# A hybrid attention and state space layer: the two gates are computed inside the state space stage, in a written-out order

## The chip, the cores and the metric

One Trainium2 chip, of which the kernel uses one core. The metric is the device time in microseconds (us) of one execution of the program, the median over repeated runs. TensorE (PE) multiplies, VectorE (DVE), ScalarE (ACT) and GpSimd (POOL) work element by element, SyncE (SP) issues the DMAs.

## The reference, cut to what matters

One layer over 1024 tokens of width 1024, all in float32:

```
xn = RMSNorm(h)
z  = xn @ W_in  -> [q | k | v | gate_attn | u_ssm | gate_ssm]     (each 512 wide)
attn = dilated_window_attention(q, k, v) * silu(gate_attn)         (8 heads of 64)
ssm  = S5(u_ssm) * silu(gate_ssm)                                  (32 groups of 16 channels, 64 complex states)
h  = h + concat(attn, ssm) @ W_out
h  = h + sigmoid(RMSNorm(h) @ W_g) * (p @ W_p)
```

S5 is a diagonal complex recurrence along the tokens: per group an input matrix, a scan, an output matrix, a skip term, then GELU and a gated linear unit.

## The kernel before, in words

The program is one function, `hybrid_layer`, unrolled completely. A scheduler sorts the instructions before the run: each engine gets a fixed order, chosen from each instruction's priority (its place in the program text, moved ahead by `tc.high_priority(offset=...)`) and from the times at which its own clock model believes that operands are ready. `AHEAD` is such an offset. Nothing is reordered on the chip: an engine whose next instruction waits, waits.

Every large product is done in three matmuls (`mm3`, L109 to L112): high part times high part, low times high, high times low. A weight block of 512 columns comes in eight pieces (`load_w`, L149 to L165): a DMA into one of three raw buffers, the high part copied by ACT (L160), the low part subtracted by DVE or POOL (L161; a string such as `GL = "QV"` says who: Q is POOL, V is DVE). The eight pieces have eight buffers (`wp`), so a block's piece can be loaded when the last matmul of the block before it that uses this piece is done.

The stages, in the order of the text:

- **u** (L193 to L235): x comes in, is split into `xh` and `xl`, and u = W_in(2048..) x is accumulated. `stats` (L179) makes 1/rms of every token from the squares: as a column per token block (`rcol`, L182 to L185) and, through the PE, as a row on all partitions (`rrow`, L189 to L191). Beside it DVE computes the small parameters of the state space part (L247 to L415).
- **state space** (L437 to L603): u is scaled by `rrow` into `ust` (L445, half by POOL, half by DVE) and goes through memory into another layout, `ut` (L510). Then 32 groups are handled in eight halves of four groups: index f (0 to 3) times h2 (0, 1). `ssm_kernels(f)` builds for both halves of f the matrices `g` (L477 to L479) and `cpw` (L482 to L484); the PE transposes g into the bank `gp` (L493) and multiplies into the bank `kp` (L489); ACT copies `gt` (L496); the convolution matrix goes through memory into `wt` (L504). `ssm_scan` makes a phase table `tc`, `tf` (L531 to L535), the PE product `vp` (L540), and on DVE and POOL the products, the scan (L548) and `xpv` (L555). `ssm_out` sums three products per group into `yp` (L570 to L572) and ACT applies GELU (L574); `ssm_store` transposes on the PE (L581) and stores. The loop at L589 to L602 runs nine steps: scan of half i, output of half i-1, and at every even i the kernels of the next f.
- **gates** (L606 to L615): first gate_ssm (columns 2560..), then gate_attn (columns 1536..). Each is eight tiles (4 feature blocks f, 2 token halves n) of 24 matmuls (`feat_tile`, L420) in the PSUM tag `big`, which has two banks. DVE multiplies a tile by `rrow` (L613) into a buffer of the tag `ev`, which has four buffers and which the eight `ust` tiles use as well; ACT applies SiLU in place (L614); a DMA stores it (`sg_s`, `sa_s`). These matmuls come later in the text than the state space stage, so the scheduler may put them into its gaps.
- **q, k, v, attention, GLU, output products, second gate** (L620 to the end). The first matmuls of q stand right behind the gates. In `attention`, `output(b)` (L730 to L740) takes the finished token block b: a DMA loads its gate `ga` from `sa_s` (feature by token, 512 byte pieces), the PE transposes the block (L736) into a bank of the tag `t` (two banks), DVE multiplies it by the gate, ACT copies the high part (L709) and POOL subtracts the low part (L710, by `EA`).

Of the kernel before, what the change touches and what calls it, by code (L numbers as in the profile page):

```python
# [15 lines left out]
OP = mybir.AluOpType  # L16
# [9 lines left out]
GL = "QV"  # L26
UE = "QV"
# [32 lines left out]
SB = (2, 1, 1, 1, 4, 6, 4, 6)  # L60
# [20 lines left out]
def hybrid_layer(ctx: ExitStack, tc: tile.TileContext, a: dict, dbg=None):  # L81
    nc = tc.nc
    V, A, Q, T = nc.vector, nc.scalar, nc.gpsimd, nc.tensor
# [21 lines left out]
    sa_s = dr.tile([512, S], F32, name="sa_s")  # L105
# [73 lines left out]
    def stats(ss, name, out_col, out_row):  # L179
# [5 lines left out]
        V.tensor_copy(out_col, r)  # L185
        for n in range(2):
# [280 lines left out]
    def ssm_kernels(f):  # L467
        wt = s2.tile([P, 8, P], F32, tag="wt", name=f"wt{f}", bufs=SB[1])
        fr = slice(f * P, (f + 1) * P)
        gts, cps = [], []  # L470
        kp = bank("pv", f"kp{f}")
        for h2 in range(2):
            gs = slice(8 * f + 4 * h2, 8 * f + 4 * h2 + 4)
            nm = f"_{f}{h2}"
            g = q4("g" + nm, (P, 4, 8, 16), "g", SB[2])
            w = q4("gw" + nm, (P, 4, 9, 16), "cw", SB[3])
            Q.tensor_tensor(g, over_l(rows(pa, 0, 8, gs), 8), over_c(ba[:, gs], 8), op=OP.mult)  # L477
            E[SE[0]].tensor_tensor(w[:, :, 0:8], over_l(rows(pb, 0, 8, gs), 8), over_c(bb[:, gs], 8), op=OP.mult)
            E[SE[1]].tensor_tensor(g, g, w[:, :, 0:8], op=OP.add)  # L479
            cpw = q4("cp" + nm, (P, 4, 9, 16), "cp", SB[4])  # L480
            w = q4("cw" + nm, (P, 4, 9, 16), "cw", SB[3])
            Q.tensor_tensor(cpw, over_l(rows(pa, 0, 9, gs), 9), over_c(cre[:, gs], 9), op=OP.mult)  # L482
            E[SE[2]].tensor_tensor(w, over_l(rows(pb, 0, 9, gs), 9), over_c(cim[:, gs], 9), op=OP.mult)
            E[SE[3]].tensor_tensor(cpw, cpw, w, op=OP.add)  # L484
            cps.append(cpw)
            for j in range(4):
                A.activation(bm[h2][:, j, 16 * j:16 * j + 16], g[:, j, 0, :], AF.Copy)
            for j in range(4):
                T.matmul(kp[64 * h2:64 * h2 + 64, 0:P], bm[h2][:, j, :],  # L489
                         cpw[:, j, 0:8, :].rearrange("p l c -> p (l c)"), start=j == 0, stop=j == 3)  # L490
            gp = bank("t", "gp" + nm)
            for j in range(4):
                T.transpose(gp[:, j * P:(j + 1) * P], g[:, j].rearrange("p l c -> p (l c)"), ident)  # L493
            gt = [q4(f"gt{ri}" + nm, (P, 4, P), "gt", SB[5]) for ri in range(2)]
            for ri in range(2):
                A.activation(gt[ri].rearrange("p g (u s) -> p g u s", u=2),  # L496
                             gp.rearrange("p (g s) -> p g s", g=4)[:, :, 64 * ri:64 * ri + 64].unsqueeze(2)
                             .to_broadcast([P, 4, 2, 64]), AF.Copy)
            gts.append(gt)
        stt(kz[:, 112:128], eye16, dsk[:, f:f + 1], kp[:, 0:16], OP.mult, OP.add)  # L500
        A.activation(kz[:, 128:240], kp[:, 16:P], AF.Copy)
        nc.sync.dma_start(k_s[fr], kz)
        for jr in range(8):
            nc.sync.dma_start(wt[16 * jr:16 * jr + 16],  # L504
                              k_s[fr, 16 * jr:16 * jr + P].rearrange("(g c) f -> c g f", c=16))
        return gts, cps, wt
# [7 lines left out]
    def ssm_scan(f, h2, gts, cps, ut):  # L514
        g0 = 8 * f + 4 * h2
        gs = slice(g0, g0 + 4)
        nm = f"_{f}{h2}"
        gt, uth = gts[h2], ut[:, 4 * h2:4 * h2 + 4]
# [17 lines left out]

        vp = [bank("s", f"vp{ri}" + nm) for ri in range(2)]
# [52 lines left out]
    for i in range(9):  # L590
# [5 lines left out]
        if i:  # L596
# [4 lines left out]
            if h2:  # L601
                ssm_store(f, ygt[f])  # L602
# [496 lines left out]
```

## Time and profile before

| what | value |
|---|---|
| median of 3 runs | 697.68 us (694.65 to 699.17) |
| the profiled execution, its own time | 699.63 us |
| its span, first to last instruction | 697.9 us |
| mean granted TensorE clock | 0.965 of full speed |
| busy PE, DVE, ACT, POOL | 643.9, 454.4, 293.1, 298.2 us |
| instructions | 11020 |

All times below are on the axis of the profiled execution, us from the start of its span. A busy PE is not a PE at its peak: the ends of matmuls are modelled, and neighbours overlap. So the pace of a run of matmuls is read from the distance between the starts of two of them. PE matmuls in full float32 stand as two instructions each.

### The profile page before, as it was taken

What the parts mean: (1) busy time and instruction counts of PE and PEld (TensorE: products, weight loads), DVE (VectorE), ACT (ScalarE), POOL (GpSimd) and SP (SyncE); (2) the same over time, 40 slices, a digit from 0 to 9 for tenths busy, and PEclk for the clock granted to TensorE, in tenths of its full rate; (3) what the DMA queues carried; (4) which work ended last, traced back from release to release, by engine and by line L of the source; (5) the groups of instructions that cost most, each with busy time, mean ns of one, the idle gap of its engine ahead of it and who ended that gap; (6) DMA issues with size and microseconds to landing.
All of it is one profiled execution on the core that took longest, in us unless ns stands there. A gap on an engine that the chain in (4) does not pass through costs nothing.

```text
span 697.9 us, 11020 instructions
## 1 busy us (share of the span) xinstructions
PE 643.9 (92%) x3964; PEld 508.5 (73%) x3964; DVE 454.4 (65%) x916; ACT 293.1 (42%) x568; POOL 298.2 (43%) x259
## 2 busy tenths in 40 slices
PE   9999498779799999999999789889999999999997
PEld 6877387668688888887767466557677888888786
DVE  5999799978721347667563899966944765625222
ACT  7532152666841323337542665533622456103210
POOL 4425855877610212314242764622332436343631
PEclk9989799999999999999999979888999999999999
DMA  7804521244854315744671868798996344014101
GB/s 250 239 7 122 147 95 53 67 53 103 177 69 68 112 64 117 181 91 104 162 131 36 217 154 156 183 216 184 215 231 221 113 150 125 27 62 152 60 31 60
DMA packets 158118, 87.25 MB, mean 125 GB/s; under 512 B 117232, under 2 KB 130416, under 8 KB 158064
## 3 DMA queue, kind: packets, MB, share of 16 engines
q1 hardware_dynamic: 158064, 86.56, 51.3%
q8 instruction: 31, 0.51, 0.3%
q14 instruction: 23, 0.19, 0.1%
HBM read 48.81 MB, written 17.27 MB: 95 GB/s over the span
## 4 chain that ended last, share of the span: by engine, by line
PE 57%; DVE 19%; DMA 10%; issue 5%; POOL 4%; ACT 4%; SPq 0%; DVEq 0%; POOLq 0%; ACTq 0%
PE gt L111 4%; PE gt L112 4%; PE gt L110 4%; PE g L111 3%; PE g L112 3%; PE g L110 3%; DMA pt<-hl 3%; DMA wr<-in_w_in 2%; PE q L111 2%; PE q L112 2%; PE q L110 2%; PE os L110 2%; PE os L112 2%; PE os L111 2%; PE oa L110 2%
## 5 line engine op out<-in xcount | busy, mean ns | idle before, releaser
L161 POOL TENSOR_TENSOR wl<-wr,wh 128x512 fp32r<-128x512 f32 x34 | 48.0, 1411 | 114.1 <-ACT wh L160 59.6
L160 ACT ACTIVATE wh<-wr 128x512 fp32r<-128x512 f32 x68 | 42.2, 626 | 51.9 <-DMA wr<-in_w_in 24.1
L783 POOL TENSOR_TENSOR hl<-p,hl 128x384 f16<-128x384 f32 (+2 forms) x34 | 39.5, 1165 | 55.4 <-ACT hl L780 17.1
L110 PE MATMUL g<-xh,wh 128*128 128x512 f32 x128 | 52.5, 410 | 10.9 <-DVE gate L613 9.8
L776 ACT ACTIVATE p<-p,st 128x384 f32<-128x384 f32 (+4 forms) x64 | 39.8, 622 | 42.1 <-DVE st L753 42.0
L111 PE MATMUL g<-xl,wh 128*128 128x512 f32 x128 | 52.8, 412 | 0.0
L112 PE MATMUL g<-xh,wl 128*128 128x512 f32 x128 | 52.4, 409 | 0.0
L110 PE MATMUL gt<-hh,wh 128*128 128x512 f32 (+1 forms) x136 | 51.8, 382 | 0.1
L111 PE MATMUL gt<-hl,wh 128*128 128x512 f32 (+1 forms) x136 | 51.7, 381 | 0.0
L112 PE MATMUL gt<-hh,wl 128*128 128x512 f32 (+1 forms) x136 | 51.2, 383 | 0.0
L161 DVE TENSOR_TENSOR wl<-wr,wh 128x512 fp32r<-128x512 f32 x34 | 30.4, 893 | 28.0 <-ACT wh L160 23.3
L989 ACT ACTIVATE gg<-gg 128x512 f32<-128x512 f32 (+1 forms) x17 | 10.1, 606 | 66.6 <-DVE gg L286 66.5
L110 PEld LDWEIGHTS g<-xh,wh 128*128 128x128 f32 x128 | 25.0, 195 | 17.1 <-DVE gate L613 10.2
L991 POOL TENSOR_TENSOR gg<-gg,hs 128x512 f32<-128x512 f32 x14 | 18.1, 1297 | 43.0 <-DVE gg L286 41.4
L613 DVE TENSOR_TENSOR gate<-g,rrow 128x512 f32<-128x512 f32 x16 | 10.9, 684 | 36.0 <-PE g L112 32.1
L286 DVE TENSOR_TENSOR gg<-gt,rrow 128x512 f32<-128x512 f32 (+1 forms) x17 | 10.8, 656 | 32.8 <-PE gt L112 32.7
L753 DVE CUSTOM_DVE_ANT_0 p<-sc,mask,gc 128x128 f32<-128x128 f32 (+3 forms) x56 | 24.3, 458 | 9.0 <-PE sc L766 5.5
L110 PEld LDWEIGHTS gt<-hh,wh 128*128 128x128 f32 x136 | 25.6, 188 | 5.8 <-ACT wh L163 0.5
L111 PEld LDWEIGHTS gt<-hl,wh 128*128 128x128 f32 x136 | 25.6, 188 | 5.4
L112 PEld LDWEIGHTS gt<-hh,wl 128*128 128x128 f32 x136 | 25.6, 188 | 5.4
L111 PEld LDWEIGHTS g<-xl,wh 128*128 128x128 f32 x128 | 25.1, 196 | 5.8 <-issue 0.3
L112 PEld LDWEIGHTS g<-xh,wl 128*128 128x128 f32 x128 | 24.9, 195 | 5.6
(300 smaller groups left out, 1949.5 us busy)
## 6 DMA issues: line engine op xcount, KB each, us to landing
wr<-in_w_in SPq DMA_DIRECT2D x48, 256.0 KB, 3.3
xr<-in_x SPq DMA_DIRECT2D x16, 256.0 KB, 5.0
wr<-in_w_out SPq DMA_DIRECT2D x16, 256.0 KB, 3.6
xos<-in_x SPq DMA_DIRECT2D x16, 256.0 KB, 4.1
h_s<-xos SPq DMA_DIRECT2D x16, 256.0 KB, 3.7
xoa<-h_s SPq DMA_DIRECT2D x16, 256.0 KB, 2.8
wr<-in_w_ple_gate SPq DMA_DIRECT2D x16, 256.0 KB, 3.0
out_t<-gg SPq DMA_DIRECT2D x15, 256.0 KB, 2.0
```

The costliest lines, as they stand in the source:

```text
L110: T.matmul(o, lh, rh, start=first, stop=False)
L111: T.matmul(o, lh, rl, start=False, stop=False)
L112: T.matmul(o, ll, rh, start=False, stop=last)
L160: A.activation(hi, raw, AF.Copy)
L161: E[lo_on[k % len(lo_on)]].tensor_tensor(lo, raw, hi.bitcast(F32), op=OP.subtract)
L286: V.tensor_tensor(o, x, y, op=op)
L613: V.tensor_tensor(gt_, o, rrow[:, n * 512:(n + 1) * 512], op=OP.mult)
L753: V.tensor_tensor_reduce(out, sc, msk, gm, init, op0=OP.add, op1=OP.min, accum_out=acc_[:, hd:hd + 1])
L776: A.activation(pb_, pb_, AF.Exp, bias=mx[:, hc], scale=-1.0, accum_out=dn[:, hc])
L783: E[LE[b][h0 % len(LE[b])]].tensor_tensor(hl[:, na:2 * na], pr_[:, 0:na], hl[:, 0:na], op=OP.subtract)
L989: A.activation(gt_, gt_, AF.Sigmoid)
L991: (V if last else Q).tensor_tensor(gt_, gt_, hs, op=OP.add)
```

## The change

1. **A fixed order for TensorE.** A small class stands in front of the tensor engine; while `T.held` is true, every matmul and transpose is told to keep the order of the text. It is set before the first gate tile and cleared after the state space loop.
2. **The gates move into the stage.** A generator `gates()` makes one piece per call: first gate_attn in seven pieces (token blocks 0 and 1 together, then 2 to 7), then gate_ssm in eight tiles. `fill()` calls it: once before the rows of 1/rms are made, three times before `ust`, once between the kernels of halves 0 and 1, once in each step of the loop, once more in steps 0 and 1.
3. **gate_attn token by token.** Its tiles have tokens on the partitions (`tok_tiles`), so 1/rms is a scale per partition, and ACT applies it with SiLU straight from PSUM; `sa_s` is stored by token block. Its eight low parts of weights are all POOL's (`GLA = "Q"`).
4. **1/rms in two pieces.** `stats_cols` stays where it was, ahead; `stats_rows` comes after the first piece of gate_attn, with no raised priority.
5. **The loop per half.** `ssm_kernels` is cut into `kern_build(i)` (POOL, DVE, ACT) and `kern_pe(i)` (PE and the copies behind it); the table is its own function; a half's kernels are built two steps ahead and its table one step ahead.
6. **Buffers.** `gt` from 6 to 4, the shared work tag `tt` from 6 to 8.
7. **In `output(b)`** POOL multiplies the token block by the gate ahead of the transposes (`EA`), and DVE subtracts the low part from PSUM afterwards.

```diff
+    class T:
+        held = False
+        @staticmethod
+        def matmul(*args, **kw):
+            i = nc.tensor.matmul(*args, **kw)
+            if T.held:
+                tc.keep_in_program_order(i)
...
+    def gates():
+        w = [load_w(wp, a["w_in"], k, 1536, lo=GLA) for k in range(KT)]
+        for bs in ((0, 1), (2,), (3,), (4,), (5,), (6,), (7,)):
+            for b, o in zip(bs, tok_tiles(w, bs, [f"ga{b}" for b in bs], "big")):
+                gt_ = ev(f"gate_a{b}")
+                with tc.high_priority(offset=AHEAD):
+                    A.activation(gt_, o, AF.Silu, scale=rcol[:, b:b + 1])
+                nc.sync.dma_start(sa_s[b], gt_)
+            yield
+        w = [load_w(wp, a["w_in"], k, 2560, lo=GL) for k in range(KT)]
+        for f in range(4):
+            for n in range(2):
+                o = feat_tile(w, f, n, "big", f"gs{f}{n}")
...
+    T.held = True
+    fill()
+    stats_rows("st1", rcol, rrow)
...
+    fill(3)
     for f in range(4):
         ust = [ev(f"ust{f}{e}", (P, 4, P)) for e in range(2)]
...
+    gcp = {i: kern_build(i) for i in range(2)}
+    tabs = {0: table(0)}
+    inp = {0: ssm_inputs(0)}
+    gt = {0: kern_pe(0, *gcp[0])}
+    fill()
+    gt[1] = kern_pe(1, *gcp[1])
     for i in range(9):
         if i < 8:
-            xpv[i] = ssm_scan(f, h2, *ker[f][:2], inp[f])
-            if not h2 and f < 3:
-                ker[f + 1], inp[f + 1] = ssm_kernels(f + 1), ssm_inputs(f + 1)
+            f = i // 2
+            if i % 2 == 0 and f < 3:
+                inp[f + 1] = ssm_inputs(f + 1)
+            vp3 = scan_pe(i, gt[i], inp[f])
+        fill()
+        if i < 8:
+            xpv[i] = ssm_scan(i, vp3, *tabs[i], gcp[i][1])
+        if i + 2 < 8:
+            gcp[i + 2] = kern_build(i + 2)
+        if i + 1 < 8:
+            tabs[i + 1] = table(i + 1)
         if i:
...
+            ssm_out(f, h2, xpv[i - 1], ygt[f], gcp[i - 1][1], inp[f], wts[f])
             if h2:
                 ssm_store(f, ygt[f])
+        if i < 2:
+            fill()
+        if i + 2 < 8:
+            gt[i + 2] = kern_pe(i + 2, *gcp[i + 2])
+    fill(16)
+    T.held = False
     sp.close()
-    for c0, dst in ((2560, sg_s), (1536, sa_s)):
-        w = [load_w(wp, a["w_in"], k, c0, lo=GL) for k in range(KT)]
...
-            nc.sync.dma_start(gl, sa_s.rearrange("(r p) t -> p r t", p=P)[:, :, b * P:(b + 1) * P])
+            nc.sync.dma_start(gl, sa_s[b].rearrange("p (r t) -> p r t", r=4))
+            E[EA[b % 2]].tensor_tensor(at_, at_, gl, op=OP.mult)
             tp = bank("t", f"at{b}").rearrange("p (r t) -> p r t", t=P)
             for j in range(4):
                 T.transpose(tp[:, j], at_[:, j], ident)
-            tt(gl, tp, gl, OP.mult)
...
-            split(*(t_[:, b % 4] for t_ in ma[n]), gl.rearrange("p r t -> p (r t)"), E[EA[b % 2]])
+            split(*(t_[:, b % 4] for t_ in ma[n]), tp.rearrange("p r t -> p (r t)"), V)
```

`kern_pe(i)` issues the four transposes into `gp`, the two copies `gt`, then the eight matmul instructions into `kp`, and for odd i the stores and loads that make `wt`. `scan_pe(i)` issues the sixteen matmul instructions into `vp`. The engines that do the element work of a half (`SE`) are unchanged.

## Rows read from the trace of the kernel before

**Rows 1.** The page, part 1: busy us, share of the span, instructions.

```profile
PE 643.9 (92%) x3964; PEld 508.5 (73%) x3964; DVE 454.4 (65%) x916; ACT 293.1 (42%) x568; POOL 298.2 (43%) x259
```

**Rows 2.** Busy time by stage: stretch, length, engines' busy us, clock, DMA, GB/s.

```profile
94.00:192.00 98.00, 82.44 (x526) 70.79 (x525) 82.84 (x101) 61.05 (x126) 69.01 (x58) 0.97 0.42 86
192.00:238.00 46.00, 46.00 (x228) 38.20 (x227) 8.77 (x14) 13.06 (x21) 5.45 (x6) 1.00 0.45 73
238.00:345.00 107.00, 107.00 (x478) 85.53 (x477) 66.08 (x193) 48.44 (x95) 30.55 (x26) 1.00 0.53 121
345.00:530.00 185.00, 167.25 (x1693) 120.41 (x1692) 136.73 (x324) 85.42 (x190) 79.57 (x63) 0.94 0.79 174
```

**Rows 3.** Timeline of TensorE, last run of u: start, us, instruction.

```profile
48.15 0.40 PE L110 MATMUL u<-xh,wh 128*128 128x512 f32 x1
...
58.19 0.39 PE L111 MATMUL u<-xl,wh 128*128 128x512 f32 x1
```

**Rows 4.** The tile q: matmul ns min/median/max, first and last start.

```profile
L110 PE MATMUL q<-wh,xh x64: 391/397/400, 238.1 to 282.4; 128*128 128x512 f32 x64
```

**Rows 5.** Waits of TensorE from 58 to 240: us in total, times, longest.

```profile
PE g L110 <- DVE gate L613: 9.8, 1, 9.8
PE kp L489 <- DVE cp L484: 8.9, 5, 3.8
PE yt L581 <- ACT ygt L574: 3.5, 1, 3.5
```

**Rows 6.** Busy time around the longest wait: columns as in Rows 2.

```profile
72.50:83.77 11.27, 1.50 (x7) 0.88 (x6) 7.46 (x21) 0.88 (x1) 9.61 (x7) 0.78 0.52 153
83.77:94.00 10.23, 10.23 (x34) 8.13 (x35) 10.13 (x11) 2.20 (x7) 6.96 (x6) 0.74 0.59 191
```

**Rows 7.** Timeline of TensorE: the small products of the state space stage.

```profile
94.19 0.60 PE L493 MATMUL gp<-ident,g 128*128 128x128 f32 x4
...
96.11 1.09 PE L489 MATMUL kp<-cp,bm 128*64 128x128 f32 x8
...
121.50 1.95 PE L540 MATMUL vp<-ut,gt 128*128 128x128 f32 x16
...
195.02 0.38 PE L570 MATMUL yp<-wt,ut 128*128 128x128 f32 x2
...
200.15 0.39 PE L572 MATMUL yp<-cpi,xpv 128*128 128x128 f32 x2
...
205.50 1.03 PE L581 MATMUL yt<-ident,ygt 128*128 128x128 f32 x8
```

**Rows 8.** Groups of DVE from 58 to 240: busy us, mean ns, idle before.

```profile
L548 DVE TENSOR_TENSOR_SCAN y<-magp,w 128x128 f32<-128x128 f32 x32 | 14.0, 496 | 2.4 <-POOL xpv L554 2.4
...
L613 DVE TENSOR_TENSOR gate<-g,rrow 128x512 f32<-128x512 f32 x16 | 10.9, 684 | 36.0 <-PE g L112 32.1 <-POOL g L477 3.8
...
L161 DVE TENSOR_TENSOR wl<-wr,wh 128x512 fp32r<-128x512 f32 x9 | 7.4, 824 | 9.2 <-ACT wh L160 9.2
...
L286 DVE TENSOR_TENSOR wf<-vp,tf 128x512 f32<-128x512 f32 x8 | 5.5, 683 | 0.9 <-ACT tf L535 0.6 <-PE vp L540 0.3
```

**Rows 9.** Groups of POOL from 58 to 240, columns as in Rows 8.

```profile
L161 POOL TENSOR_TENSOR wl<-wr,wh 128x512 fp32r<-128x512 f32 x9 | 12.3, 1362 | 48.2 <-PE g L111 37.3 <-ACT wh L160 11.0
...
L445 POOL TENSOR_TENSOR ust<-uraw,rrow 128x256 f32<-128x256 f32 x8 | 11.2, 1426 | 4.6 <-DVE rrow L191 3.1 <-DMA u_s<-ust 1.6
```

**Rows 10.** Timeline of ACT: one change of its function table.

```profile
143.02 1.28 ACT L614 ACT_TABLE_LOAD   x1
144.31 0.63 ACT L614 ACTIVATE gate<-gate 128x512 f32<-128x512 f32 x1
```

**Rows 11.** The tile ga, the attention gate: ns min/median/max, first and last start.

```profile
L286 DVE TENSOR_TENSOR ga<-at,ga x8: 678/689/693, 393.9 to 525.6; 128x512 f32<-128x512 f32 x8
...
L710 POOL TENSOR_TENSOR mal<-ga,mah x8: 1282/1298/1672, 440.8 to 527.1; 128x512 fp32r<-128x512 f32 x8
```

**Rows 12.** Waits of DVE from 340 to the end.

```profile
DVE ga L286 <- DMA ga<-sa_s: 5.5, 3, 2.2
```

More of the change, by code (lines that the diff above doesn't have):

```diff
@@ L26 @@
 GL = "QV"
+GLA = "Q"
 UE = "QV"
@@ L233, in hybrid_layer, with feat_tile, ev, wa @@
     with tc.high_priority(offset=AHEAD):
-        stats(ss, "st1", rcol, rrow)
+        stats_cols(ss, "st1", rcol)
         V.tensor_tensor(rsq_, rcol, rcol, op=OP.mult)
+    def feat_tile(w, f, n, tag, name):
+        o = bank(tag, name)
+        c = slice(n * 512, (n + 1) * 512)
+        for k in range(KT):
+            mm3(o, w[k][0][:, f * P:(f + 1) * P], w[k][1][:, f * P:(f + 1) * P],
+                xh[k][:, c], xl[k][:, c], k == 0, k == KT - 1)
+        return o
+    def ev(name, shape=(P, 512)):
+        return rp.tile(list(shape), F32, tag="ev", name=name, bufs=4)
+    def wa(name, shape, dt=F32):
+        return rp.tile(list(shape), dt, tag="wa", name=name, bufs=2)
+    def wb(name, shape, dt=F32):
+        return wbp.tile(list(shape), dt, tag="wb", name=name, bufs=2)
+    def tok_tiles(w, bs, names, tag):
+        os_ = [bank(tag, name) for name in names]
+        for k in range(KT):
+            for o, b in zip(os_, bs):
+                c = slice(b * P, (b + 1) * P)
+                mm3(o, xh[k][:, c], xl[k][:, c], w[k][0], w[k][1], k == 0, k == KT - 1)
+        return os_
+    def gates():
[11 more added lines that the diff above has]
+                o = feat_tile(w, f, n, "big", f"gs{f}{n}")
+                gt_ = ev(f"gate_s{f}{n}")
+                with tc.high_priority(offset=AHEAD):
+                    V.tensor_tensor(gt_, o, rrow[:, n * 512:(n + 1) * 512], op=OP.mult)
+                    A.activation(gt_, gt_, AF.Silu)
+                nc.sync.dma_start(sg_s[f * P:(f + 1) * P, n * 512:(n + 1) * 512], gt_)
+                yield
+    gates_ = gates()
+    def fill(n=1):
+        for _ in range(n):
+            next(gates_, None)
+    T.held = True
+    fill()
+    stats_rows("st1", rcol, rrow)
     def p16(name):
@@ L465, in over_c @@
         return x.unsqueeze(2).to_broadcast([P, 4, n, 16])
-    def ssm_kernels(f):
-        wt = s2.tile([P, 8, P], F32, tag="wt", name=f"wt{f}", bufs=SB[1])
-        fr = slice(f * P, (f + 1) * P)
[L470 to L506, printed above, removed]
@@ new lines, in kern_pe @@
+    def kern_pe(i, g, cpw):
+        f, h2 = divmod(i, 2)
+        nm = f"_{f}{h2}"
+        fr = slice(f * P, (f + 1) * P)
+        gp = bank("t", "gp" + nm)
+        for j in range(4):
+            T.transpose(gp[:, j * P:(j + 1) * P], g[:, j].rearrange("p l c -> p (l c)"), ident)
+        gt = [q4(f"gt{ri}" + nm, (P, 4, P), "gt", SB[5]) for ri in range(2)]
+        for ri in range(2):
+            A.activation(gt[ri].rearrange("p g (u s) -> p g u s", u=2),
+                         gp.rearrange("p (g s) -> p g s", g=4)[:, :, 64 * ri:64 * ri + 64].unsqueeze(2)
+                         .to_broadcast([P, 4, 2, 64]), AF.Copy)
+        if not h2:
+            kps[f] = bank("pv", f"kp{f}")
+        kp = kps[f]
+        for j in range(4):
+            T.matmul(kp[64 * h2:64 * h2 + 64, 0:P], bm[h2][:, j, :],
+                     cpw[:, j, 0:8, :].rearrange("p l c -> p (l c)"), start=j == 0, stop=j == 3)
+        if h2:
+            stt(kz[:, 112:128], eye16, dsk[:, f:f + 1], kp[:, 0:16], OP.mult, OP.add)
+            A.activation(kz[:, 128:240], kp[:, 16:P], AF.Copy)
+            nc.sync.dma_start(k_s[fr], kz)
+            wts[f] = s2.tile([P, 8, P], F32, tag="wt", name=f"wt{f}", bufs=SB[1])
+            for jr in range(8):
+                nc.sync.dma_start(wts[f][16 * jr:16 * jr + 16],
+                                  k_s[fr, 16 * jr:16 * jr + P].rearrange("(g c) f -> c g f", c=16))
+        return gt
@@ L511, in ssm_inputs, with table @@
         return ut
[L514 to L518, printed above, removed]
+    def table(i):
+        gs = slice(4 * i, 4 * i + 4)
+        nm = f"_{i // 2}{i % 2}"
         tc_, tf = q4("tc" + nm, tag="e", bufs=SB[6]), q4("tf" + nm, tag="e", bufs=SB[6])
```

79 lines of the change are left out of this document (39 added, 40 removed).

## The prediction

> **What bounds the kernel now.** I read the page first: TensorE is busy for 92% of the span and every other engine for two thirds or less [rows 1]. That says which engine matters, but not where it loses time, so the next view is the busy time by stage. From 238 to 345 TensorE is busy in every microsecond, at clock 1.00; from 192 to 238 too, while DVE does 8.77 us of work in 46 [rows 2]. From 94 to 192 it is busy 82.4 of 98, and DVE 82.8 of 98 as well. So there are two pieces of one large stage: first the state space work, where DVE sets the pace and gate matmuls fill TensorE's gaps only in part, then the rest of the gates, where TensorE is alone. Work that TensorE does in that tail could have stood in the gaps in front of it.
>
> How large are the gaps? The pace of the big matmuls: from 48.15 to 58.19 lie 43 steps, 0.2335 us each [rows 3]. One more matmul follows, so u ends at about 58.65, and q begins at 238.1 [rows 4]: the stage lasts 179.4 us. TensorE's work in it, at full pace:
> - gates: 16 tiles of 24 matmuls, 384 x 0.2335 = 89.7;
> - `yp`: 195.02 to 200.15 are 23 steps of a pair, 0.223 each; 12 pairs a half, 2.68; eight halves 21.4 [rows 7];
> - a pair lasts 0.38, so one instruction lasts 0.27 beyond the start of the last. `vp`, 16 instructions at 0.1115: 1.78, by eight 14.3. `kp`: (1.09 - 0.27)/7 = 0.117, eight of them 0.94, by eight 7.5. `gp`: (0.60 - 0.27)/3 = 0.11, four 0.44, by eight 3.5. `yt`: (1.03 - 0.27)/7 = 0.109, eight 0.87, by four 3.5. The rows of 1/rms, 16 instructions at the pace of `kp`: 1.9.
>
> The sum is 141.8, so 37.6 us of the stage are not work. The three longest of ten kinds of waits are 9.8 for a gate tile's DVE multiply, 8.9 for DVE's sum `cp`, 3.5 for GELU [rows 5]. The rest is small waits and slow clock: after the 9.8 us the granted clock averages 0.74 over 83.77 to 94, part of it at the lower level of 1.2 GHz, and 34 matmuls that need 7.9 us take 10.2 [rows 6].
>
> **The change, part by part.** I follow TensorE, whose order is now the order of the text, and put a wait wherever the next instruction can be late.
>
> Start. Blocks 0 and 1 of gate_attn (48 matmuls, 11.2 us) come right behind u. They need the two `big` banks, which ACT has to empty, and weights whose low parts are now POOL's alone: eight by 1.36 = 10.9 us where POOL had four [rows 9], while DVE is rid of four by 0.82 [rows 8]. Value 3 us of wait, between 0 and 7 (five extra subtractions on POOL if all of it showed). End 72.9. Then the rows of 1/rms, 1.9: 74.8, later than before, when nothing stood between u and them. What hides that: `ust` needs them, 8 by 1.43 = 11.4 us on POOL [rows 9], which ends near 87; then half 0's `g` and `cp` follow, near 92. TensorE meanwhile does blocks 2 to 4 (16.8 us), until 91.6. The 9.8 us wait can't come back here: SiLU now reads PSUM itself, DVE's multiply L613 is gone for gate_attn (8 by 0.684 = 5.5 us off DVE, rows 8), and its `ev` buffers are asked for ahead of `ust`'s.
>
> Kernels 0 and 1 with block 5 between: 1.4 + 5.6 + 1.4. If POOL is late with `ust`, the wait falls here: value 2, between 0 and 5. End 102.
>
> Loop. 38.3 of the 141.8 are then done, 103.5 are left. A step with kernels takes TensorE 1.78 + 5.6 + 2.68 + 0.44 + 1.38 = 11.9 us; steps 0 and 1 have a gate tile more. DVE's nine groups of a half (the eleven rows from the scan to `wf`, without L613 and L161) sum to 87.5 us, 10.9 a half [rows 8], and with a gate tile's 0.68 it is 11.6. So the two engines are level, and DVE's own gaps decide. Before, DVE was busy for 85% of 94 to 192 [rows 2]; at that share a half would take 11.6/0.85 = 13.6, 1.7 more than TensorE's, in the four steps 2 to 5 together 6.8. Steps 0, 1, 6 and 7 have room (more matmuls there, or less DVE work). Value 6, between 0 (the two-step lead covers it) and 15 (twice that share of gaps). The buffers `g` and `cw` stay single, so DVE can't run further ahead; that excludes a gain beyond 0.
>
> The weights change once inside the loop, from gate_attn to gate_ssm, before step 1's tile: eight loads with ACT, DVE and POOL all in use. TensorE has 3.2 us of other work there. Value 3, between 0 and 8 (four of POOL's subtractions of 1.36 late, and two of its 1.4 us operations in front).
>
> The tail: output 7, its transposes, then q, whose weights can only be loaded behind the last gate tile. 3.6 us of TensorE's work and some 14 us for loading stand side by side, with DVE and POOL nearly free. Before, q's memory was free long before q; now it is given back just ahead of it, but the first tile of q is not read until 11 us after q starts. Value 2, between 0 and 6.
>
> SP's queue gets the same DMAs in another order; the stores of gates wait there for SiLU and stand in front of `wt`'s loads. From the last use of `wt` to its next TensorE has 0.9 + 1.4 + 1.8 + 5.6 = 9.7 us of other work, so I put nothing, inside the 15 above.
>
> ACT: in 94 to 192 it is busy for 61.05 us, 7.6 a half [rows 2]; one SiLU (0.63) and one table load (1.28) more in each step make 9.5, under 11.9. After a load the next instruction starts 1.29 us behind the load's start [rows 10], so a change of table costs the load alone. Nothing on the path.
> The Trainium skill ("ScalarE: Activation LUTs", What ACT_TABLE_LOAD costs) speaks against that: it adds a drain of about 1.38 us to each load. By it ACT would need about 12.3 us a step and set the pace; the trace of this kernel shows no such gap, and I take the trace.
>
> Waits together: 3 + 2 + 6 + 3 + 2 = 16. The stage ends at 58.65 + 141.8 + 16 = 216.5 instead of 238.1: 21.6 us earlier. Shorter waits also mean less slow clock; I leave that inside the bounds.
>
> Behind the stage. q and k run without a gap until 345 [rows 2], so the shift passes through. In the attention DVE's multiply from PSUM (0.69) becomes a subtraction from PSUM, which I price the same; POOL's subtraction (1.30) becomes a multiplication of the same size [rows 11]. What moves is a wait: DVE stood 5.5 us for the gate's load [rows 12], now POOL does. TensorE is busy 167 of 185 us there, so little of it returns: a gain of 1, between a gain of 5.5 and a loss of 5.5 (POOL, waiting, holds attention's subtractions that are queued behind).
>
> Sum against the profiled execution: 699.63 - 21.6 - 1 = 677.0. The median of the runs lies 1.95 lower than that execution, so the forecast is **675 us**.
>
> **The rivals.**
> - *Better than that.* The lead of two steps covers DVE's gaps and waits shrink to 5: 32.6 + 1 off, 664. For it: DVE loses over 9 us of work. Against it: single `g` and `cw`.
> - *Half of it.* Only the 9.8 us wait and the 2.3 us of slow clock behind it go, and the waits for `cp` come back in the new order: 12.1 off, 686. For it: the same engines feed the same products. Against it: a gate tile now stands between any two of them. ACT as the pace setter ends here too: with a change of table twice as long as its row, ACT needs 9.5 + 2 x 1.28 = 12.1 a step, at DVE's share of 85% 14.2, which is 2.3 more than TensorE; in the six steps that hold a gate tile and GELU 14 us in place of DVE's 6, so 683, chance 0.02. That is the mechanism of the page named above.
> - *Nothing.* The order only changes which instruction waits. All 37.6 us come back: 698. For it: 82.8 of 98 us of DVE; against it: the last 46 us before q need no DVE, so they can move.
> - *Slower.* Place: each half's kernels on TensorE. Now nothing may pass them. If DVE's sum `cp` is late by its longest wait of 3.8 us [rows 5] in each of eight halves, and each wait costs slow clock in the proportion of rows 6 (2.3 to 9.8, so 0.9), that is 37.6; with the 10 us of the other waits the end is 58.65 + 141.8 + 47.6 = 248: 10 us slower, 708. It decides from 4.1 us a half on, all included. For it: DVE is level with TensorE. Against it: kernels are started a step and a half before they are needed.
>
> **How the numbers follow.** Chances: the forecast, 668 to 682, 0.48; better, below 668, 0.12; half, 682 to 691, 0.17; nothing, 691 to 705, 0.13; slower, above 705, 0.10. A run of this kernel tells about 1% from no change, here 7 us. Faster by over 1% (below 690.7): 0.48 + 0.12 + 0.17 = 0.77; within 1%: 0.13; slower: 0.10. With all waits at their lower ends, and the attention's best, the time would be 655; at their upper ends (41 us of waits, 5.5 in the attention) 707. The range that leaves out 2 in 10: 662 to 694, which gives up 0.05 below and about 0.15 above.
>
> **What would show it.** Right: q's first matmul near 216; the wait of g for L613 gone; no stretch of 32 us before q with DVE idle; steps of the loop 12 to 14 us apart; DVE's wait for `ga` gone, POOL's in its place. Wrong: first matmuls of half 0's kernels later than 97; a wait of TensorE for DVE in every step; gate_ssm's first tile waiting for POOL's or DVE's low parts for over 8 us; q later than 230; the time from q's first matmul to the end other than 460 by more than 6 us.

## The result, and the profile after

The changed kernel takes 723.99 us (median of 4 runs, 718.29 to 726.85) beside 698.42 of the kernel before in the same rounds: 1.034 times as long, 95% interval 1.030 to 1.038. The forecast was 675 and its range ended at 694. The profiled execution of the changed kernel has a span of 725.1 us at a mean clock of 0.938, against 697.9 at 0.965.

Part 1 of the page after, which answers to [rows 1]:

```profile
PE 652.3 (90%) x3964; PEld 515.3 (71%) x3964; DVE 434.9 (60%) x904; ACT 299.0 (41%) x571; POOL 302.0 (42%) x263
```

TensorE runs the same 3964 instructions; it lost 27 us by waiting and by lower clock. Where, the first matmuls of the tiles say. The tile q after, which answers to [rows 4]:

```profile
L92 PE MATMUL q<-wh,xh x64: 392/397/479, 250.9 to 296.1; 128*128 128x512 f32 x64
```

q begins at 250.9, 12.8 us later than before, where 21.6 earlier was forecast. The same row of other tiles, for every kernel of this study, gives this table (us). Here glu is the first matmul of the GLU, os and oa those of the output products of the state space and the attention half, and gt that of the second gate's PSUM tiles (not the copies `gt` of the state space stage); the three columns with "to" are differences of these starts.

| kernel | first gp | q | glu | glu to os | os to oa | oa to gt | span |
|---|---|---|---|---|---|---|---|
| before | 94.2 | 238.1 | 386.1 | 54.0 | 90.6 | 38.5 | 697.9 |
| after | 108.4 | 250.9 | 398.5 | 61.5 | 93.2 | 43.2 | 725.1 |
| e1_ust_first | 95.6 | 233.0 | 381.2 | 62.7 | 91.8 | 43.1 | 707.5 |
| e2_store_late | 109.1 | 223.1 | 378.4 | 63.6 | 92.8 | 42.5 | 706.2 |
| e3_gate_alone | 93.1 | 236.4 | 382.6 | 62.2 | 91.8 | 41.8 | 707.4 |
| e4_no_hold | 106.3 | 219.7 | 376.2 | 62.0 | 91.6 | 42.8 | 701.7 |
| e5_both | 95.2 | 206.4 | 361.9 | 63.6 | 92.9 | 42.9 | 689.9 |
| e6_feature | 95.8 | 224.2 | 373.1 | 54.1 | 91.7 | 38.2 | 685.9 |
| e7_no_mult | 92.1 | 235.6 | 384.1 | 57.4 | 87.1 | 37.2 | 694.4 |
| e8_feature_free | 97.8 | 223.1 | 371.7 | 54.1 | 90.3 | 38.7 | 683.3 |
| e9_mult_dve | 95.0 | 205.8 | 361.7 | 60.7 | 85.2 | 42.8 | 678.9 |
| e10_mult_dve_free | 93.7 | 204.7 | 360.1 | 61.0 | 85.6 | 42.6 | 678.1 |
| e11_mult_half | 95.4 | 206.4 | 362.2 | 59.9 | 88.9 | 41.3 | 681.2 |
| e12_best | 95.5 | 206.3 | 362.3 | 61.5 | 87.7 | 43.3 | 683.5 |

In some kernels, the changed one among them, the last small products of the state space stage stand among q's matmuls, so glu is the fairer mark for that stage. From the first gt to the end every kernel takes 128.5 to 129.1 us. So the 27.2 us that the change added are 12.4 up to glu and 14.8 from glu to gt (183.1 before, 197.9 after): two separate losses. Each of e1 to e11 is one execution, and the changed kernel's profiled execution is the slowest of its four: two executions of one program, e9 and e12, lie 3.8 us apart from glu to gt, so a difference of a few us between two rows can't be told from none.

**Up to glu.** TensorE's waits from 55 to 260 in the kernel after, which answer to [rows 5] (us in total, times, longest):

```profile
PE yt L98 <- ACT ygt L643: 13.2, 3, 4.9
PE gp L98 <- issue: 12.2, 1, 12.2
PE ga L92 <- ACT uraw L251: 6.7, 1, 6.7
PE kp L92 <- DVE cp L539: 2.5, 1, 2.5
PE gs L92 <- POOL wl L178: 0.8, 1, 0.8
PE gp L98 <- ACT yo L653: 0.8, 1, 0.8
```

The waits of [rows 5] for the gate tile and for `cp` have gone or shrunk. Two that were small or absent are the largest now. The first to show, the 12.2 us in front of `gp`, in TensorE's timeline after:

```profile
95.75 0.40 PE L92 MATMUL ga<-wh,xl 128*128 128x512 f32 x1
108.37 1.09 PE L98 MATMUL gp<-ident,g 128*128 128x128 f32 x4 [12.22 <-issue]
111.95 1.94 PE L92 MATMUL kp<-cp,bm 128*64 128x128 f32 x8 [2.49 <-DVE cp L539]
...
120.85 0.60 PE L98 MATMUL gp<-ident,g 128*128 128x128 f32 x4
```

From the end of the fifth token block, at 96.0, to half 1's transposes at 120.85 lie 24.85 us, for 7.0 us of work (0.44 and 0.94 for half 0's products, 5.6 for a block, by the prediction's paces): 17.9 lost. These transposes read `g`, whose sum DVE ended at 108.27, 0.1 ahead of them:

```profile
106.56 1.71 DVE L534 TENSOR_TENSOR g<-g,gw 128x512 f32<-128x512 f32 x1
```

`g` does not read `ust`, but it stands behind it on DVE and POOL, and `ust` was late. POOL's timeline and SP's queue after, in the same stretch:

```profile
80.42 1.43 POOL L504 TENSOR_TENSOR ust<-uraw,rrow 128x256 f32<-128x256 f32 x2 [11.58 <-DMA sa_s<-gate_a]
93.45 1.42 POOL L504 TENSOR_TENSOR ust<-uraw,rrow 128x256 f32<-128x256 f32 x2 [11.60 <-DMA sa_s<-gate_a]
100.10 1.40 POOL L504 TENSOR_TENSOR ust<-uraw,rrow 128x256 f32<-128x256 f32 x2 [5.23 <-DMA u_s<-ust]
...
104.13 1.61 POOL L532 TENSOR_TENSOR g<-pa,ba 128x512 f32<-128x512 f32 x1 [0.76 <-DVE ust L504]
```

```profile
77.54 19.73 SPq L289 DMA_DIRECT2D sa_s<-gate_a  x5
97.37 7.00 SPq L507 DMA_DIRECT2D u_s<-ust  x8
```

`ust` has its row of 1/rms and its engines free at 80, and waits all the same, for stores of the attention gate. Both take their buffers from the tag `ev`, four of them, in turn. The gate's blocks 0 to 4 stand ahead of `ust` in the text, so `ust` gets a buffer when a gate block has been computed, passed through SiLU and stored; and all eight stores of `ust` stand in SP's queue behind five stores that wait for matmuls as late as 95.75. DVE meanwhile stands still:

```profile
DVE ust L504 <- DMA sa_s<-gate_a: 18.3, 2, 10.2
```

The second wait, `yt`, in ACT's and TensorE's timelines after, at its longest:

```profile
198.33 0.63 ACT L298 ACTIVATE gate_s<-gate_s 128x512 f32<-128x512 f32 x1 [3.11 <-DVE gate_s L297]
200.08 0.63 ACT L596 ACTIVATE tf<-tc 64x512 f32<-64x512 f32 x1 [1.12 <-POOL tc L595]
200.72 0.63 ACT L597 ACTIVATE tf<-tc 64x512 f32<-64x512 f32 x1
201.37 1.28 ACT L643 ACT_TABLE_LOAD   x1
202.66 0.66 ACT L643 ACTIVATE ygt<-yp 128x256 f32<-128x256 f32 x2
```

```profile
203.37 1.97 PE L98 MATMUL yt<-ident,ygt 128*128 128x128 f32 x8 [4.90 <-ACT ygt L643]
205.29 1.11 PE L98 MATMUL gp<-ident,g 128*128 128x128 f32 x4
206.33 1.97 PE L92 MATMUL kp<-cp,bm 128*64 128x128 f32 x8
```

In the text the transposes `yt` stand right behind the products `yp` whose GELU they need. Nothing else may pass, so TensorE stands for the whole chain on ACT: a wait for POOL's part of the next table (1.12 us), two copies of that table, the load of the function table, the GELU. Then it comes back with the clock partly at the lower of its two levels, 1.2 GHz (0.66 granted from 200 to 210): eight `yt` take 1.97 us and eight `kp` too, where [rows 7] have 1.03 and 1.09.

The third, 6.7 us at the start, in ACT's timeline after:

```profile
62.40 0.63 ACT L177 ACTIVATE wh<-wr 128x512 fp32r<-128x512 f32 x1 [2.89 <-DMA wr<-in_w_in]
62.94 1.07 ACT L251 ACTIVATE uraw<-u 128x512 f32<-128x512 f32 x2
```

The last copies of u, which free the banks for the gate's first blocks, stand behind a copy of a gate weight that waits for its load. What held that load back was not traced.

Busy time by stage after, columns as in [rows 2]:

```profile
58.00:72.00 14.00, 8.43 (x26) 6.70 (x27) 13.69 (x31) 4.99 (x9) 9.67 (x7) 0.76 0.30 95
72.00:96.00 24.00, 24.00 (x112) 19.44 (x110) 6.96 (x16) 2.75 (x4) 2.85 (x4) 1.00 0.12 45
96.00:121.00 25.00, 10.29 (x39) 8.03 (x39) 17.37 (x16) 6.89 (x18) 17.34 (x13) 0.66 0.45 136
121.00:251.00 130.00, 114.98 (x670) 98.99 (x668) 67.25 (x104) 70.12 (x131) 71.40 (x62) 0.92 0.39 85
```

From 72 to 96 TensorE is full and DVE works 6.96 of 24 us: work that was to be done beside the gate's blocks was shut out. In the loop DVE is busy for 67 of 130: it does not set the pace there.

**From glu to gt.** Busy time in the three stretches glu to os, os to oa, oa to gt; the kernel before first, then the kernel after:

```profile
386.10:440.10 54.00, 44.49 (x439) 30.56 (x437) 53.57 (x104) 33.31 (x72) 35.09 (x27) 0.91 0.78 169
440.10:530.70 90.60, 85.06 (x1009) 61.05 (x1009) 64.26 (x169) 37.30 (x81) 32.58 (x26) 0.92 0.95 211
530.70:569.20 38.50, 37.47 (x166) 30.22 (x166) 23.66 (x30) 17.08 (x28) 11.64 (x9) 1.00 0.47 151
```

```profile
398.50:460.00 61.50, 50.05 (x476) 33.21 (x474) 57.83 (x112) 35.77 (x77) 41.93 (x31) 0.86 0.74 174
460.00:553.20 93.20, 82.91 (x983) 60.10 (x982) 60.59 (x161) 34.66 (x76) 26.25 (x21) 0.91 0.87 188
553.20:596.40 43.20, 39.97 (x165) 32.11 (x164) 21.96 (x30) 17.35 (x29) 12.63 (x10) 0.92 0.42 135
```

DVE's busy time over the three is 141.5 before and 140.4 after, POOL's 79.3 and 80.8: the work is the same, its place is not. The first stretch, in which DVE was busy for 53.57 of 54.00 us before, has gained 6.8 us of POOL, 5.7 of them four of the multiplications. The tiles `atok` and `mal` after, which answer to [rows 11]:

```profile
L802 POOL TENSOR_TENSOR atok<-atok,ga x8: 1274/1288/1706, 406.0 to 539.6; 128x512 f32<-128x512 f32 x8
```

```profile
L778 DVE TENSOR_TENSOR mal<-at,mah x8: 672/676/692, 458.8 to 548.0; 128x512 fp32r<-128x512 f32 x8
```

Each operation lasts what its counterpart lasted. But POOL's eight now stand in front of the transposes, from 406.0 on; before, POOL's eight stood behind everything of their block, from 440.8 on.

### The profile page after: what moved, and what is told of

Same layout as the page of the kernel before. It is cut to its first block, busy times and chain, and to the rows that moved or that the text cites. A ratio compares the mean times of both kernels' runs of the same rounds, so it can differ in the third digit from the quotient of the medians.

```text
span 725.1 us, 11010 instructions
## 1 busy us (share of the span) xinstructions
PE 652.3 (90%) x3964; PEld 515.3 (71%) x3964; DVE 434.9 (60%) x904; ACT 299.0 (41%) x571; POOL 302.0 (42%) x263
## 4 chain that ended last, share of the span: by engine, by line
PE 60%; DMA 12%; DVE 12%; issue 5%; ACT 5%; POOL 5%; SPq 1%; DVEq 0%; ACTq 0%; POOLq 0%
PE gt L92 10%; PE ga L92 7%; PE q L92 6%; PE oa L92 6%; PE os L92 6%; PE k L92 5%; DMA pt<-hl 4%; PE gs L92 3%; PE pe L92 3%; DMA wr<-in_w_in 3%; PE v L92 2%; PE vp L92 2%; PE pv L92 2%; PE sc L92 2%; DMA wr<-in_w_out 1%
## 5 line engine op out<-in xcount | busy, mean ns | idle before, releaser
L178 POOL TENSOR_TENSOR wl<-wr,wh 128x512 fp32r<-128x512 f32 x38 | 56.6, 1495 | 76.4 <-ACT wh L177 76.4
L92 PEld LDWEIGHTS <-pt 128*128 128x128 f16 (+1 forms) x888 | 26.7, 101 | 24.9 <-DMA pt<-hl 13.9
L178 DVE TENSOR_TENSOR wl<-wr,wh 128x512 fp32r<-128x512 f32 x30 | 26.3, 877 | 28.9 <-ACT wh L177 26.6
L92 PE MATMUL pv<-vv,pt 128*128 128x64 f16 x504 | 25.5, 202 | 10.8 <-DMA pt<-hl 9.9
L92 PE MATMUL ga<-wh,xh 128*128 128x512 f32 x64 | 27.4, 428 | 6.7 <-ACT uraw L251 6.7
L92 PE MATMUL sc<-ks,qh 128*32 128x128 f16 (+4 forms) x160 | 24.8, 272 | 6.5 <-DVE st L821 6.3
L361 DVE TENSOR_TENSOR gg<-gt,rrow 128x512 f32<-128x512 f32 (+1 forms) x17 | 10.7, 655 | 32.7 <-PE gt L92 32.6
L850 DVE CAST hl<-p 128x384 f16<-128x384 f32 (+2 forms) x34 | 20.2, 597 | 16.5 <-DMA pt<-hl 12.0
L92 PE MATMUL os<-msh,wh 128*128 128x512 f32 x64 | 27.9, 435 | 2.3 <-DVE xos L372 2.3
L92 PE MATMUL oa<-mah,wh 128*128 128x512 f32 x64 | 26.7, 416 | 3.2 <-DVE xoa L372 3.2
L1013 POOL TENSOR_TENSOR ssb<-ssb,xoa 128x512 f32<-128x512 f32 x12 | 16.0, 1333 | 30.0 <-ACT xoa L1012 30.0
```

The costliest lines, as they stand in the source:

```text
L92: i = nc.tensor.matmul(*args, **kw)
L178: E[lo_on[k % len(lo_on)]].tensor_tensor(lo, raw, hi.bitcast(F32), op=OP.subtract)
L361: V.tensor_tensor(o, x, y, op=op)
L850: V.tensor_copy(hl[:, 0:na], pr_[:, 0:na])
L1013: E[SB2[f]].tensor_tensor(ssb[:, c], ssb[:, c], xr, op=OP.add)
```

## The experiments

**e1_ust_first: three gate blocks behind the stacks.** The changed kernel; blocks 2 to 4 come after `ust` in the text, so only the first piece of the gate (blocks 0 and 1) stands ahead of `ust`.

```diff
-    fill(3)
     for f in range(4):
         ust = [ev(f"ust{f}{e}", (P, 4, P)) for e in range(2)]
...
+    fill(3)
     xrp.close()
```

> The changed kernel with one line moved: the three gate_attn blocks 2 to 4 are asked for behind the ust loop, not ahead of it; TensorE's order stays as it was. Theory (the eight ust tiles stand behind five gate tiles in the four ev buffers and in SP's queue): ust ends near 91 in place of 104, the first transposes of the kernels come at about 96 in place of 108.4, the wait of 12.2 us is gone, and with the slow clock behind it about 16 us are saved: q's first matmul near 235 in place of 250.9, span near 709. Rival (POOL and DVE are late with ust and g in any case, since 1/rms comes 14 us later than before): the first transposes stay later than 103 and less than 7 us are saved, span over 718.

Measured: 709.29 us. The first `gp` stands at 95.6 instead of 108.4, q at 233.0. SP's queue in e1:

```profile
77.12 1.02 SPq L289 DMA_DIRECT2D sa_s<-gate_a  x2
81.62 7.23 SPq L506 DMA_DIRECT2D u_s<-ust  x8
```

The stores of `ust` begin at 81.6 behind two of the gate, not at 97.4 behind five. glu comes 17.3 us earlier, so the 17.9 lost between the blocks go with this order. It sets the turn of the buffers and the turn in SP's queue at once; which of the two would have been enough was not tried.

**e2_store_late: the store a step later.** The changed kernel; `yt` of a finished tile come behind the next step's gate tile, so that GELU has time.

```diff
         fill()
+        if i > 2 and i % 2:
+            ssm_store(i // 2 - 1, ygt[i // 2 - 1])
         if i < 8:
             xpv[i] = ssm_scan(i, vp3, *tabs[i], gcp[i][1])
...
-            if h2:
-                ssm_store(f, ygt[f])
...
     fill(16)
+    ssm_store(3, ygt[3])
     T.held = False
```

> The changed kernel with ssm_store of a feature block moved one step on, behind the next step's gate tile, so that TensorE has 8.8 us of other work between the products yp and the transposes yt. Theory (the fixed order puts yt right behind yp, and TensorE stands for GELU and its table load, 13.2 us in three waits, with about 11 us of slow clock behind them): the waits of yt for ygt fall under 1 us, the loop from the first vp (122.4) to q (250.9) shrinks from 128.5 to about 106, span near 703. Rival (DVE or ACT sets the pace of the loop): other waits of the same size take their place, the loop stays over 120 and the span over 717.

Measured: 707.96 us, 19 less than after; the span, 706.2, is 3 above the one expected, and the rival is out. glu comes 20.1 us earlier, though waits for `yt` were only 13.2. Busy time of e2 over its loop and the start of q:

```profile
121.00:229.00 108.00, 105.47 (x652) 90.60 (x650) 66.83 (x104) 66.92 (x127) 71.26 (x61) 1.00 0.38 95
```

The clock is 1.00 where it was 0.92: with the waits the slow stretches behind them are gone too.

**e3_gate_alone: the token-major gate without the rest.** The kernel before, its order of stages kept (the gates behind the state space stage), with gate_attn by `tok_tiles` (tokens on the partitions: token-major) and SiLU from PSUM, `sa_s` by token block, and the new `output(b)`.

```diff
-    for c0, dst in ((2560, sg_s), (1536, sa_s)):
...
+    for bs in ((0, 1), (2,), (3,), (4,), (5,), (6,), (7,)):
+        for b, o in zip(bs, tok_tiles(w, bs, [f"ga{b}" for b in bs], "big")):
...
+            E[EA[b % 2]].tensor_tensor(at_, at_, gl, op=OP.mult)
```

> The kernel before with only the token-by-token attention gate and the new order in output(b): gates behind the state space stage as before, no fixed order, no new loop. Theory (POOL's multiplication by the gate stands in the stretch in which DVE and POOL are full, where before its subtraction came later): from q's first matmul to the end 470 to 475 us in place of 459.8, the stage ahead of q 176 to 180, span 706 to 712. Rival (the 14 us behind q come from elsewhere, as from another schedule): 458 to 463 behind q, span 692 to 699.

Measured: 709.42 us. q stands at 236.4 and the rest takes 471.0 (707.4 - 236.4), both as expected. With no pipeline and no fixed order at all, glu to gt takes 195.8 us instead of 183.1. So 12.7 of the second loss's 14.8 us come with the token-major form: its gate blocks, its loads and the new `output(b)`, taken together.

**e4_no_hold: no fixed order.** The changed kernel with the tie left out.

```diff
-    T.held = True
+    T.held = False
```

> The changed kernel with TensorE free of the order of the text; all else as changed. Theory (the order of the text is what makes TensorE wait for GELU, but not what makes ust late): the yt waits fall from 13.2 to under 5 us, the wait ahead of the first kernel transposes stays above 8 us or is filled by gate matmuls, q's first matmul at 235 to 243, span 707 to 717. Rival (the fixed order costs nothing, the new loop and the buffers do): q near 251 and span near 725.

Measured: 703.55 us, better than the theory allowed: q at 219.7, 23.3 us less than after in all. The waits for `yt` are 0.8, as expected. The theory had left open whether gate matmuls would fill the first hole, and its time had not counted on it. They do; busy time of e4 there:

```profile
96.00:121.00 25.00, 22.30 (x110) 17.61 (x109) 19.36 (x17) 9.84 (x23) 23.04 (x17) 1.00 0.63 187
```

`gp` is as late as in the kernel after (106.3), since the buffers bind still (POOL's `ust` waits 19.8 us for stores of the gate), but the scheduler put gate matmuls in front of it: 22.3 us busy of 25 where after has 10.3. The tie turned both late operands into idle time. That is not all that they cost: e5, which keeps the tie and mends the operands, has glu 14.3 us earlier than e4.

**e5_both: e1 and e2 together.**

> The changed kernel with both moves: blocks 2 to 4 of the gate behind the u stacks, and the store of a tile's y one step later. Theory (the two losses are separate, one before the loop and one inside it): against 726.85 the first move gave 17.6 us and the second 18.9, so together 36.5: 690 us; the first transposes of the half kernels near 96, no wait of TensorE for ygt above 2 us, and the glu stretch begins near 362. Rival (both moves free the same cover, TensorE meets the next engine, VectorE or GpSimd, as soon as one of them is made): above 699, with a wait of TensorE for cp, xpv or g of over 8 us in total. In both cases the stretch from the first glu matmul to the first os matmul stays at 61 to 64.

Measured: 691.68 us. glu at 361.9 is 36.6 earlier than after, and 17.3 + 20.1 is 37.4: the two losses add, no other engine came up behind them. TensorE's two longest waits from 55 to 260 in e5:

```profile
PE ga L92 <- ACT uraw L251: 6.5, 1, 6.5
PE ga L92 <- ACT gate_a L288: 0.9, 1, 0.9
```

The largest is the start's. glu stands 24.2 earlier than before, so the stage does what was forecast of it (21.6) once two orders in the text are mended.

**e6_feature: e5 with the attention gate feature-major (features on the partitions).** Gate blocks and `output(b)` as in the kernel before, the row of 1/rms ahead of the first block.

```diff
+    stats_rows("st1", rcol, rrow)
     fill()
-    stats_rows("st1", rcol, rrow)
...
-            E[EA[b % 2]].tensor_tensor(at_, at_, gl, op=OP.mult)
...
+            tt(gl, tp, gl, OP.mult)
```

> e5_both with the attention gate feature-major again, in the gate's blocks and in the attention's output, as in the kernel before; the row of 1/rms is made ahead of the first block, which needs it. Theory (the token-major form costs some 12 to 13 us behind q, as the gate alone showed: 8 from glu to os, 1 from os to oa, 4 from oa to gt): 677 us, range 671 to 684, glu to os 53 to 56, os to oa 90 to 91, oa to gt 38 to 39; VectorE has 8 x 0.65 us more in the state space stage, which hides. Rival (the stretch behind glu is long because of what the pipeline leaves behind for it, not because of the gate's form): glu to os stays above 60 and the time above 686.

Measured: 687.71 us, above the range expected. Behind glu the theory holds in full: 54.1, 91.7 and 38.2, the numbers of the kernel before. What it took for hidden was not: glu stands 11.2 us later than in e5. Waits of TensorE from 55 to 260 in e6:

```profile
PE ga L92 <- DVE gate_a L291: 5.4, 2, 3.3
PE st1r L92 <- issue: 4.6, 1, 4.6
PE gs L92 <- ACT wh L177: 4.1, 1, 4.1
```

All waits of this stretch sum to 17.1 us in e6 and to 10.9 in e5: e6 waits for the row of 1/rms (4.6, in place of e5's 6.5 at the start), for DVE's multiply, and 5.8 where the weights change. From 55 to 96 its clock is 0.83, where e5 has 0.92. So the token-major form earns some 11 us in the stage and pays more behind it; how the 11 divide was not tried.

**e7_no_mult: e3 without the multiplication by the gate.** The load of the gate is left out with it: the attention's output is ungated.

```diff
-            gl = b3[0].tile([P, 4, P], F32, tag="ga", name=f"ga{b}", bufs=GA)
-            nc.sync.dma_start(gl, sa_s[b].rearrange("p (r t) -> p r t", r=4))
-            E[EA[b % 2]].tensor_tensor(at_, at_, gl, op=OP.mult)
```

> The kernel before with the token-major gate alone (e3), without the multiplication by the attention gate and its load: the attention's output is left ungated. Theory (GpSimd's multiplications, 4 of 1.35 us in the glu stretch where VectorE and GpSimd are both full, are what makes it longer): glu to os falls from 62.3 to 54 to 57 and the time from 709.4 to 699 to 704. Rival (it is the hi/lo split out of the transposes' bank on VectorE, and the outputs' place ahead of other work): glu to os stays above 60, time above 707.

Measured: 696.21 us, 3 below the range expected, and 57.4 from glu to os, just above it. Busy time of e7 in the three stretches:

```profile
384.10:441.50 57.40, 44.50 (x445) 29.80 (x444) 57.19 (x107) 34.43 (x75) 36.69 (x27) 0.91 0.75 160
441.50:528.60 87.10, 82.35 (x1004) 59.48 (x1003) 58.88 (x165) 35.41 (x79) 22.56 (x17) 0.96 0.94 198
528.60:565.80 37.20, 37.20 (x166) 30.22 (x165) 24.47 (x31) 17.49 (x29) 11.65 (x9) 1.00 0.47 151
```

The total 181.7 is 14.1 less than e3: without POOL's eight multiplications (8 x 1.35 = 10.8 us of POOL) and their loads the second loss is gone. The split on DVE from PSUM is still there, so it is not what costs. But e7 gates nothing, and has eight operations on POOL fewer than the kernel before for its 1.4 us less (181.7 against 183.1); so it doesn't tell whether the multiplications cost by their place or by their mere time on POOL. The place that the theory named was too narrow: the gain is 4.8, 4.7 and 4.6 in the three stretches, not most of it in the first.

**e8_feature_free: e6 without the tie.**

> e6_feature without the tie of TensorE to program order. Theory (with both moves made nothing stands in TensorE's way, so the fixed order neither costs nor gains): within 4 us of e6_feature. Rival one (the planner still fills holes that the fixed order leaves): 5 to 12 us faster. Rival two (the planner puts the gate's blocks ahead and leaves the small products bare): over 5 us slower.

Measured: 685.09 us, 2.6 less than e6. With both holes closed the tie costs next to nothing.

**e9_mult_dve: e5 with the multiplications on DVE.**

```diff
-EA = "QQ"
+EA = "VV"
```

> e5_both with the eight multiplications by the attention gate on VectorE in place of GpSimd. Theory (what the token-major form costs is GpSimd's time in the stretch where both engines are full: without the multiplication glu to gt fell from 196 to 182 us, 14.4 for 8 x 1.38 = 11 us of GpSimd): VectorE pays 8 x 0.69 = 5.5 us alone, glu to gt falls from 199.4 to 187 to 192 and the time from 691.7 to 680 to 685. Rival (VectorE is the fuller of the two in that stretch, and its eight more instructions cost as much as GpSimd's): glu to gt stays above 196, time 688 or more.

Measured: 680.81 us, glu to gt 188.7, both as expected. The first stretch gives 2.9 us and the second 7.7; the third stays at 42.8. The third takes 37.2 to 38.7 only in the kernels in which nothing multiplies ahead of the transposes (before, e6, e7, e8), and 41.3 or more in all others, whichever engine multiplies. So part of the loss goes with the engine and part stays with the token-major form.

**e10_mult_dve_free: e9 without the tie.**

> e9_mult_dve without the tie of TensorE to program order. Theory (with the stacks and the store moved nothing is left for the tie to cost): within 4 us of e9_mult_dve, as between the feature-major pair (687.7 and 685.1). Rival (with the token-major blocks first the planner spends them at once and leaves the small products of the later halves bare): glu's first matmul later than 366 and over 5 us slower.

Measured: 679.89 us: no difference that one execution can show.

**e11_mult_half: every second multiplication on DVE.**

> e5_both with every second multiplication by the attention gate on VectorE. Theory (each multiplication taken from GpSimd gives some 1.0 to 1.5 us): between e5_both and e9_mult_dve, 685 to 689. Rival (the two engines balance, and half on each is the best): below e9_mult_dve by over 2 us.

Measured: 682.99 us, below the expected range. From glu to gt it takes 190.1, between e9's 188.7 and the 192.5 of the same program in e12, where e5 takes 199.4: with four of the eight moved, what is left can't be told from all eight moved. Which of POOL's eight hurt most was not tried.

**e12_best: e9, timed in rounds.**

> The same kernel as e9_mult_dve, timed against the kernel before in three rounds. Expected from the one execution of e9 (680.8): a median of 679 to 683 and a ratio of 0.970 to 0.980. If the single time was a lucky one, the median is above 686.

Measured: 685.74 us beside 701.63, ratio 0.976 (0.971 to 0.981). The ratio is where it was expected, the median 2.7 us above. e9's single time lies 1.3 below the fastest of these four (682.11); of the 4.6 us that the two profiled executions differ, 3.8 lie between glu and gt (192.5 and 188.7). So DVE's multiplications gain 6.9 to 10.7 us there against e5. This kernel is faster than the kernel before by 1.9 to 2.9%, and its slowest run (686.27) is below the changed kernel's fastest (718.29).

## Why the prediction was wrong

The prediction's stage was 141.8 of work and 16 of waits. After the change u ends at 56.7 (2.0 earlier than before) and q begins at 250.9 instead of 216.5, with one set of `yt`, 0.9 us of the work, still to come; so the waits and slow stretches are 53.3. The stage is 34.4 of the some 50 us that the forecast is off, and 15.8 are the stretch from glu to gt. By the prediction's terms:

- *Start, value 3, between 0 and 7.* Measured 6.7 of wait for the banks that ACT empties; what is left of the 53.3 after this wait and the two losses below (17.9 and 25.9), 2.8, goes with the slow clock behind it (0.76 from 58 to 72). The operand was the one named, the size at the upper end. The bound of 7 had another reason, though: five extra subtractions on POOL, where eight for four are four more, 5.4 us. What held the banks was ACT's order: a weight copy that waited 2.89 us for its load, ahead of the last copies of u.
- *Kernels 0 and 1, value 2, with `ust` done near 87.* This is the first step that failed: 17.9. I wrote that the gate's `ev` buffers "are asked for ahead of `ust`'s" and took it for a gain. It is the fault: four buffers handed out in turn make `ust` wait for gate stores, and DVE and POOL, which I had priced as busy with `ust`, stood idle. Of SP's queue I looked at `wt` only, not at the eight stores of `ust` that now stood behind five of the gate. The list of signs had this one: first kernels later than 97 (108.4). Two more of its signs came true: q later than 230, and 474.2 us from q to the end where 460 was to hold.
- *DVE in steps 2 to 5, value 6.* Measured nothing: one wait for `cp` of 2.5 before the loop, none for DVE inside that the list shows. The two-step lead covers DVE. *Weight switch, value 3*: 0.8. *Tail, value 2*: no wait shown. These terms were over-sized by 10.
- *GELU, no term at all.* This is the second step that failed. The wait for `ygt` stood in [rows 5] with 3.5 us in an order that the scheduler could still fill; I counted `yt` as work and asked only about operands from DVE. With the order fixed, three of the four `yt` wait for their own step's GELU: 13.2 us. The loop from its first `vp` at 122.4 to q lasts 128.5 for 102.6 of work (103.5 less the last `yt`); waits in it sum to 14.8 (13.2 and two of 0.8), and the other 11 go with the slow clock, which I had left "inside the bounds".
- *ACT.* That a table change costs its load alone holds again: GELU starts 1.29 us after the load's start, as in [rows 10]. The Trainium skill ("ScalarE: Activation LUTs", What ACT_TABLE_LOAD costs) adds a drain that this trace does not show either. But I asked whether ACT has time enough in a step (70 of 130 us busy, it has), not whether TensorE stands behind it.
- *Attention, a gain of 1, between 5.5 either way.* This is the third step that failed. DVE's wait for `ga` went and POOL's came (1.9), and the sizes of the operations are as priced, but the stretch grew by 14.8. I priced a swap of equal operations between two engines at nothing. e3 puts 12.7 us of it on the token-major form, and in e7 14.1 go when the multiplications and their loads are left out; e9 and e12 show 6.9 to 10.7 gone with the multiplications on DVE. What changed besides the engine is where POOL's operation stands: behind the transposes it delayed only its own block's product, ahead of them it delays the transposes and what DVE and POOL have queued there. That this place is the cause is argued, not shown: no run moved the place alone.

The rival "slower" had the sign and nearly the mechanism (nothing may pass a late operand in a fixed order), but at another place and price: `cp` from DVE, which was late once. It was the fixed order together with operands that I had not put on the list, `ust` through a shared buffer and `yt` through GELU. e5 and e9 show that the gain forecast in the stage was there: 24.2 us up to glu.

## What to carry to other kernels

When a fixed order is given to an engine, list every operand of every instruction that is now tied, and ask who makes it and how long after the instruction in front; a producer on an engine that is half idle is as late as any, if the instruction stands right behind its input. When a step is moved forward, look at what it shares with the step it passes: a rotating set of buffers and an in-order queue of transfers couple two stages that have no data in common. And an exchange of equal operations between two engines need not be free when one of them also moves from the end of a chain to its front: here the whole exchange cost 12.7 us.

## What was not expected of the hardware

In the loop a wait cost more than it lasted, since the stretch behind it ran at a lower granted clock: 14.8 us of waits came with some 11 of slow matmuls, and e2, which takes 13.2 of these waits away, brought glu 20.1 forward. And one and the same DVE multiplication of 128x512 took from 0.68 to 1.87 us, by what POOL did beside it. DVE's timeline and then POOL's, in e9:

```profile
379.38 0.68 DVE L803 TENSOR_TENSOR atok<-atok,ga 128x512 f32<-128x512 f32 x1
...
396.06 1.66 DVE L803 TENSOR_TENSOR atok<-atok,ga 128x512 f32<-128x512 f32 x1
```

```profile
375.96 1.27 POOL L959 TENSOR_TENSOR ym<-ym,gm 128x512 f32<-128x512 f32 x1 [0.85 <-DMA gm<-sg_s]
379.83 1.25 POOL L852 TENSOR_TENSOR hl<-p,hl 128x512 f16<-128x512 f32 x1 [2.60 <-ACT hl L849]
...
393.98 3.19 POOL L852 TENSOR_TENSOR hl<-p,hl 128x512 f16<-128x512 f32 x2
```

At 379.4 POOL is idle for most of the multiplication, at 396.1 it works until 397.2. All eight of e9 go this way: the three that start while POOL works take 1.42, 1.66 and 1.87 us, the five that start while it is idle 0.68 or 0.69. So the time that POOL's eight multiplications cost need not be all their own: beside them DVE's instructions may get longer. How the 14.1 us divide into these was not measured.
